# Moving the block sums and low parts of one stage to VectorE, and reordering loads at two stage borders, in a one-core mixer and feed-forward block

## The chip, the core and the metric

One core of a Trainium2 chip runs the whole program as one launch. The metric is device microseconds of one execution; the time before is the median of three runs, 1592.3 us (1587.58 to 1594.35). The instruction streams are TensorE (PE, with its weight loads as PEld), VectorE (DVE), ScalarE (ACT), GpSimd (POOL) and SyncE (SP). SP issues most loads and stores; POOL issues some as well. Each stream runs its own instructions strictly in the order in which they were written.

## What is computed

One layer over 1024 positions of width 1024. The reference, cut to what matters here:

```python
u = rms_norm(h, g_norm_mix)
proj = einsum('btd,de->bte', u, w_in) + b_in
mq, mk, mv, mo, mi, mf, nq, nkv, ngate, merge = split_columns(proj, IN_SIZES)
y_m = mlstm_mixer(mq, mk, mv, mo, mi, mf, ...)   # 4 heads of 128, conv of 4 taps, chunks of 128
y_n = nsa_mixer(nq, nkv, ngate, pe_cmp, ...)     # compressed, selected and window attention, 8 heads
branch = einsum('btnw,nwd->btnd', stack(y_m, y_n), w_branch)
h = h + sum_n(sigmoid(merge) * branch) @ w_out
f = rms_norm(h, g_norm_ffn)
h = h + (silu(f @ w_gate) * (f @ w_up)) @ w_down
return rms_norm(h, g_final)
```

Matrix products are done on pairs of float32r numbers, a high part (ACT copies the value in the shorter type) and a low part (value minus high part, one subtraction), as three products: high by high, high by low, low by high.

## The kernel before

The work has five stages; the times in brackets are those of the profiled execution.

**Stage A** (0 to 399 us) loads x, norms and transposes it, and computes all of the input projection but most of the merge columns, the four mLSTM heads, and the compressed keys and values. The projection goes pair by pair (`PAIRS`, twelve pairs of 256 output columns). Each pair takes seven block products instead of eight (a seven-product scheme): product 1, 2 and 4 take raw weight blocks, products 6, 7, 5 and 3 take sums and differences of blocks. `sums` (L741) forms these, `prep` (L767) makes the high part on ACT and the low part by `ew`, `product` runs 12 matmuls of 512 columns on PE, and `finish` (L797) adds the result into the output with the bias. For the query and key pairs `conv` (L838) adds the four taps: one ACT step and three DVE steps over 1024 columns. The activations' own block sums are made once by `forms` and `fsplit` (L599, L613), for j = 0 to 3.

Where `ew` is given `ANY` (L400), the step may go to DVE (one instruction, planned at 700 ns) or to POOL (two instructions of half the size, planned at 1800 ns); where it is given `V`, only to DVE.

`compress` (L1030) makes the compressed keys and values: for each of two inputs it loads four pieces of weights, adds the position rows to shifted windows (`windows`, L1047: four small additions for each piece, on DVE or POOL), and runs four small matmuls for each piece. `restore` (L1074) brings a part of the activations' parts back from memory by eight POOL loads, once product 4 of the last pair no longer needs their place. `head_load` (L1085), `values` (L1098), `mask`, `scale_q` and `core` (L1178) are the heads' recurrence. `merge_B` (L1270) fills PE beside them.

The order of stage A is worked out when the program is written: a planner (`Plan`, L64) keeps a clock for each engine, takes each step's cost and a delay for each DMA, and writes whichever step can start first; among steps that are ready it takes the lowest rank, which is the place in the program minus a boost. `load` (L406) holds the planner's picture of DMA: 1.5 us after the issue, big loads one after the other at 4 ns for each KB, POOL loads always 4.5 us.

**Stage C** (the attention from 413.7 to 736 us) goes with ten merge tiles of 48 matmuls as filler on PE, ordered by a second planner. Its keys, queries and bias rows are loaded by `load_pair` (L1354) from POOL: for the first pair of heads four loads of 256 KB for the queries (QA), eight of 256 KB for the keys (KH, KL), and four for bias rows (FB, FW). `behind(0)` (L1349) then copies the compressed keys behind them, also on POOL. The values (VHL, 2 MB, written out to memory in stage A) are loaded back by the step at L1299 to L1301, which the planner of stage A writes; so it stands in POOL's queue ahead of `load_pair(0)` (L1385). The pools of stage C reuse stage A's memory tile by tile.

**Stage D** (its branch products from 766.7 to about 860) multiplies both mixers' outputs by the branch weights and gates them. `load_y` (L1807) loads the twelve pieces of y (512 KB each) and makes their high parts on ACT and low parts on DVE; it runs step by step between the last two merge tiles, and what is left of it is run off before the first branch product. The first eight branch steps (`FIRST`, L1866) go over both halves and two column tiles for the first mixer, then the same for the second; `load_gates` (L1835) loads the merge gates, for the first four steps right before them.

**Stage E** (860 to the end) is the output projection and the feed-forward part, with the seven-product scheme again but a planner and an `ANY` of its own; the change does not touch it.

Of the kernel before, what the change touches and what calls it, by code (L numbers as in the profile page):

```python
# [14 lines left out]
P = 128  # L15
T = 1024
# [22 lines left out]
FB_ = 40  # L39
MA_ = (60, 60)  # L40
# [130 lines left out]
def body(ctx, tc, a, out, stop=None, dbg=None):  # L171
# [166 lines left out]
    with ExitStack() as sa:  # L338
# [67 lines left out]
        def load(eng, kb, parts, reads, writes, cost=450.0, after=0.0):  # L406

            q = {"SP": nc.sync, "ACT": nc.scalar, "Pool": nc.gpsimd}[eng]

            def go(e):  # L410
                for d_, s_ in parts:
                    q.dma_start(d_() if callable(d_) else d_, s_() if callable(s_) else s_)
                n = len(landed)
                if eng != "Pool":
                    if n >= 8:
                        st.end = max(st.end, landed[n - 8][0])
                    big = [x for x in landed if x[1]]
                    t = st.end + 1500.0
                    if kb > 100:
                        t = max([t] + [x[0] for x in big[-1:]]) + 4.0 * kb  # L420
                    landed.append((t, kb > 100))
                    st.lat = t - st.end
                else:
                    st.lat = 4500.0
            st = pA.step(((eng, cost),), go, reads, writes, after=after)
            return st
# [172 lines left out]
        def fsplit(q, j, src, reads):  # L599
            if q == 4:  # L600
                i = 2 * j + 1
                cs = slice(P * i, P * i + P)
                b = K(True, prior=[ub[i][0], ub[i][2]])
                hi, lo = UTH[:, 0:4, cs], UTL[:, 0:4, cs]
            else:
                b = K(True)
                hi, lo = (X[:, j, XI[q], z] for z in range(2))
                xform.append(b)
            fsb[q, j] = [b]
            act(630.0, lambda: hi, src, AF.Copy, reads, [b])  # L610
            ew(ANY, lambda: lo, src, lambda: cast32(hi), ALU.subtract, reads, [b])

        def forms(j):  # L613

            p12, p22 = ptb[2 * j + 1]
            fsb[3, j] = ub[2 * j + 1][1::2]
            ce, cs = (slice(P * n, P * n + P) for n in (2 * j, 2 * j + 1))
            us = ub[2 * j + 1][0::2]
            load("SP", 512, [(d_u[j][z], cast32((UTH, UTL)[z])[:, 0:4, cs]) for z in range(2)], us, [dub[j]])
            c, t1, t2, t4 = (piece(nm, z) for nm in ("g00", "g01") for z in range(2))  # L620
            at = lambda b: (lambda: four(b.ap))
            u_ = lambda t, kh: (lambda: cast32(t)[:, 4 * kh:4 * kh + 4, ce])
# [3 lines left out]
            ew(ANY, at(t1), at(t1), u_(UTL, 0), ALU.subtract, [l11], [t1])  # L626
            ew(V, at(t2), at(p22), at(t1), ALU.subtract, [p22, t1], [t2])
            ew(V, at(c), at(p22), at(c), ALU.subtract, [p22], [c])
            ew(ANY, at(t4), u_(UTH, 1), at(t2), ALU.subtract, [t2, h21], [t4])
            ew(ANY, at(t4), at(t4), u_(UTL, 1), ALU.add, [l21], [t4])  # L630
# [85 lines left out]

        PAIRS = [("n", 0), ("c", 0), ("q", 0), ("n", 1), ("k", 0), ("s", 0), ("q", 1), ("v", 0), ("k", 1), ("v", 1), ("o", 0), ("o", 1)]
# [23 lines left out]
        def sums(m, n):  # L741
# [5 lines left out]
            if n == 3:  # L747
                ew(ANY, h(r0, LO), h(r0, LO), h(r0, HI), ALU.subtract, (), [r0])
                o = (r0, h(r0, LO))
            elif n == 1:  # L750
                sums(m, 3)
                ew(ANY, h(r0, HI), h(r0, HI), h(r1, HI), ALU.add, [r1], [r0])
                o = (r0, h(r0, HI))
            elif n == 2:
                b = piece("x3", m % 2)
                ew(ANY, lambda: four(b.ap), h(r1, HI), sums(m, 3)[1], ALU.subtract, [r0, r1], [b])
                o = (b, lambda: four(b.ap))
            else:
                d, s2 = sums(m, 2)
                ew(ANY, h(r1, LO), h(r1, LO), s2, ALU.subtract, [d], [r1])  # L760
                o = (r1, h(r1, LO))
# [5 lines left out]
        def prep(m, q):  # L767
# [29 lines left out]
        def finish(m, blk, ps, other):  # L797
# [4 lines left out]
            pv, ov = (lambda: ps.ap), (lambda: other.ap)  # L802
            if kind in "qk":
# [4 lines left out]
                stt(800.0, lambda: par(flat(w.ap), r), lambda: four(ps.ap), bias, lambda: four(other.ap), ALU.add, ALU.add, [ps, other, b_c], [w])  # L808
# [6 lines left out]
            if kind == "o":  # L815
                ew(V, v, pv, ov, ALU.add, [ps, other], [x])
                stp("ACT", 630.0, lambda: nc.scalar.activation(x.ap, x.ap, AF.Sigmoid, bias=bias), [b_c, tabs[-1]], [x])
                store(256, [(par(d_mx["o"][j], r), lambda: four(x.ap))], x, dst["o", j])
            else:
                stt(760.0, v, pv, bias, ov, ALU.add, ALU.add, [ps, other, b_c], [x])  # L820
# [3 lines left out]
                else:  # L824
# [6 lines left out]
                    else:  # L831
                        ew(ANY, lambda: fr(x.ap), v, lambda: y.ap, ALU.subtract, [y], [x])
# [5 lines left out]
        def conv(m, col):  # L838
# [3 lines left out]
            pA.boost = -60  # L842
# [4 lines left out]
            for s in range(1, 4):  # L847
                stt(1700.0, lambda s=s: flat(c.ap)[:, s:T], lambda s=s: flat(w.ap)[:, 0:T - s], tap(3 - s), lambda s=s: flat(c.ap)[:, s:T], ALU.mult, ALU.add, [w], [c])
# [6 lines left out]
        def product(m, q, part=None):  # L855
# [28 lines left out]
            elif q == 5:  # L884
                finish(m, (1, 1), ps, v[3])
                add(v[2], v[2])
# [40 lines left out]
        seq += [(m, q) for m in range(2, NP - 1) for q in (1, 2, 6, 7, 5, 4, 3)]  # L927
        seq += [(NP - 1, q) for q in (1, 2, 4, 6, 7, 5, 3)]
# [101 lines left out]
        def compress(j):  # L1030
# [10 lines left out]
            for z in range(4):  # L1041
# [5 lines left out]
                def windows(e, z=z, fl=fl):  # L1047
                    for o in range(4 * z, 4 * z + 4):
                        ENG[e].tensor_scalar(fl()[:, o % 4], kx()[:, :, 2 * o:2 * o + 16 * 62 + 1:16], COLS[:, R_PE + 16 * j + o:R_PE + 16 * j + o + 1], None, ALU.add)
                pA.step((("DVE", 1700.0), ("Pool", 4000.0)), windows, [kb, b_c], [fb_])  # L1050
# [4 lines left out]
                stp("PE", 880.0, go, [fb_, wb], [ph])  # L1055
            stp("ACT", 330.0, lambda: nc.scalar.activation(hsv, ph.ap[:, 0:126], AF.Silu), [ph, tabs[-1]], [b_hs])
# [74 lines left out]
        for n, (m, q) in enumerate(seq):  # L1131
# [143 lines left out]
        head_load(0, "vo")  # L1275
# [22 lines left out]
        vh = {}  # L1298
        vb_ = K(None, keys=[(f"v{n}", z) for n in range(4) for z in range(2)], make=lambda: vh.setdefault("t", att.tile([P, NT, 4, P], F32R, name="VHL", tag="VHL")))  # L1299
        load("Pool", 2048, [(lambda: vb_.ap.rearrange("p i n c -> p (i n c)"), d_vh)], [b_dvh], [vb_], cost=700.0)  # L1300
# [9 lines left out]
        VHL = vh["t"]  # L1310
# [75 lines left out]
    behind(0)  # L1386

# [414 lines left out]
    with ExitStack() as se:  # L1802
# [4 lines left out]
        def load_y():  # L1807

            ring = [q1_tile(n, F32)[:, 2 * z:2 * z + 2, :].rearrange("p a c -> p (a c)") for n in (4, 0, 1) for z in range(2)]
            ys, loads = {}, 0  # L1810
            for k in range(10):
                ys[k] = []
                for src in ([d_ym[k]] if k < 4 else [d_yn[0][k - 4], d_yn[1][k - 4]]) if k < 8 else []:
                    ys[k].append(ring[loads % 6])
                    loads += 1
                    nc.sync.dma_start(ys[k][-1], src[:, :])
                if k > 1:
                    y, *more = ys.pop(k - 2)
                    for y2 in more:
                        nc.vector.tensor_tensor(y, y, y2, ALU.add)  # L1820
                    for half in range(2):
                        hs = slice(512 * half, 512 * half + 512)
                        split_evict(YH[:, k - 2, hs], YL[:, k - 2, hs], y[:, hs])
                yield

        ly = load_y()
        for j in range(NMB + NMX + NMC, 16):
            for z, _ in enumerate(merge_tile(j, gring, psD, 8)):
                if z % 2 == 1:
                    next(ly, None)  # L1830
        for _ in ly:
            pass
        sgs = {}
# [7 lines left out]
        wide = Pieces([q1_tile(n, F32)[:, z, :] for n in (5, 3) for z in range(4)])  # L1841
        gring, narrow = wide, gring
# [24 lines left out]
        for d, half, b in FIRST[:4]:  # L1867
            load_gates(d, half)
        for n, (d, half, b) in enumerate(FIRST):
# [10 lines left out]
            if n == 5:  # L1880
                gring = narrow
                gring.n = 0
                load_gates(2, 0)
        for d in range(2, 8):
# [625 lines left out]
```

## Time and profile before

| | before |
|---|---|
| median of 3 runs | 1592.3 us (1587.58 to 1594.35) |
| the profiled execution | 1597.51 us, its span 1595.7 us |
| busy in the span | PE 97%, DVE 72%, ACT 49%, POOL 19% |
| mean granted TensorE clock | 0.985 |

A page of the profile gives busy time by engine, the span in 40 slices, the chain that ended last, and the costliest groups. Other views used here: the waits (who waited for whom, summed), a table of stretches (busy time of each engine between two moments, with the granted clock), the timeline of one engine, groups by line, and the DMA issues with their time to landing. L with a number is a line of the kernel; `wOwhi<-rA,wOwhi` reads "writes wOwhi from rA and wOwhi", where whi and wlo name buffers of a ring that holds high and low parts, rA, Rg, RG and XR are buffers of stage A, X the activations' sums, and PSA its PSUM banks. XB is the memory of X in its second use. A busy PE is not PE at its peak.

### The profile page before, as it was taken

What the parts mean: (1) busy time and instruction counts of PE and PEld (TensorE: products, weight loads), DVE (VectorE), ACT (ScalarE), POOL (GpSimd) and SP (SyncE); (2) the same over time, 40 slices, a digit from 0 to 9 for tenths busy, and PEclk for the clock granted to TensorE, in tenths of its full rate; (3) what the DMA queues carried; (4) which work ended last, traced back from release to release, by engine and by line L of the source; (5) the groups of instructions that cost most, each with busy time, mean ns of one, the idle gap of its engine ahead of it and who ended that gap; (6) DMA issues with size and microseconds to landing.
All of it is one profiled execution on the core that took longest, in us unless ns stands there. A gap on an engine that the chain in (4) does not pass through costs nothing.

```text
span 1595.7 us, 22548 instructions
## 1 busy us (share of the span) xinstructions
PE 1545.5 (97%) x7810; PEld 1304.5 (82%) x7810; DVE 1149.9 (72%) x2334; ACT 779.6 (49%) x1677; POOL 304.9 (19%) x435
## 2 busy tenths in 40 slices
PE   9899999999699999999799999999999999999997
PEld 7777878888599989898688888888888888888886
DVE  6987777546498968884565678666666666988996
ACT  6533333366488868884444454333333333454443
POOL 4767665422211221101002000000000000000130
PEclk9999999999799999999899999999999999999999
DMA  7446774694722452216546423322222223741302
GB/s 205 162 128 206 214 240 130 165 267 156 158 67 90 87 136 67 83 41 204 169 143 209 137 89 123 102 83 79 80 79 79 81 91 100 283 167 45 106 1 106
DMA packets 169980, 205.86 MB, mean 129 GB/s; under 512 B 10345, under 2 KB 128391, under 8 KB 169610
## 3 DMA queue, kind: packets, MB, share of 16 engines
q1 hardware_dynamic: 156584, 179.43, 36.2%
q0 software_dynamic: 12992, 24.67, 6.6%
q8 instruction: 61, 1.00, 0.3%
q14 instruction: 53, 0.43, 0.1%
q10 hardware_dynamic: 290, 0.33, 0.1%
HBM read 149.77 MB, written 62.48 MB: 133 GB/s over the span
## 4 chain that ended last, share of the span: by engine, by line
PE 83%; DMA 7%; DVE 4%; ACT 2%; issue 2%; POOL 1%; SPq 1%; DVEq 0%; POOLq 0%; ACTq 0%
PE PS L287 14%; PE PS L288 14%; PE PS L286 14%; PE T L1504 4%; PE PSA L286 4%; PE PSA L288 4%; PE PSA L287 4%; PE d L286 2%; PE d L288 2%; PE d L287 2%; PE obank L1524 2%; PE obank L1526 2%; PE br L286 2%; PE br L287 2%; PE br L288 2%
## 5 line engine op out<-in xcount | busy, mean ns | idle before, releaser
L1942 DVE TENSOR_TENSOR sl<-PS,sl 128x512 f32<-128x512 f32 x182 | 123.6, 689 | 100.9 <-PE PS L288 100.5
L1942 POOL TENSOR_TENSOR acc<-acc 128x512 f32<-128x512 f32 x6 | 9.2, 1549 | 617.6 <-DVE acc L1942 617.6
L1513 DVE TENSOR_TENSOR TL<-T,TH 128x512 fp32r<-128x512 f32 (+1 forms) x184 | 103.1, 582 | 33.3 <-ACT TH L1509 32.1
L1942 DVE TENSOR_TENSOR sl<-sl,sl 128x512 f32<-128x512 f32 (+1 forms) x130 | 88.6, 688 | 22.9 <-DMA d_h<-sl 7.2
L1509 ACT ACTIVATE TH<-T 128x512 fp32r<-128x512 f32 (+1 forms) x184 | 90.1, 510 | 29.9 <-PE T L1504 27.3
L1945 ACT ACTIVATE sl<-sl 128x512 f32<-128x512 f32 (+1 forms) x77 | 48.5, 632 | 58.0 <-PE PS L287 34.4
L1524 PE MATMUL obank<-TH,VHL 128*128 128x256 f32 x264 | 75.4, 309 | 0.0
L286 PE MATMUL d<-UTH,whi 128*128 128x512 f32 x176 | 71.9, 409 | 1.0 <-ACT mg L1341 0.7
L288 PE MATMUL d<-UTH,wlo 128*128 128x512 f32 x176 | 69.1, 393 | 0.0
L287 PE MATMUL d<-UTL,whi 128*128 128x512 f32 x176 | 69.0, 392 | 0.0
L1526 PE MATMUL obank<-TL,VHL 128*128 128x256 f32 x264 | 68.0, 281 | 0.0
L286 PE MATMUL PS<-q 128*128 128x512 f32 x172 | 66.9, 389 | 0.0
L287 PE MATMUL PS<-q 128*128 128x512 f32 x172 | 66.9, 389 | 0.0
L288 PE MATMUL PS<-q 128*128 128x512 f32 x172 | 66.9, 389 | 0.0
L263 POOL TENSOR_TENSOR wlo<-raw,whi 128x256 fp32r<-128x256 f32 x44 | 31.1, 737 | 184.8 <-ACT whi L257 154.4
L288 PE MATMUL PSA<-UTH,wOwlo 128*128 128x512 f32 x164 | 64.8, 395 | 1.3 <-POOL wOwlo L441 1.3
L286 PE MATMUL PSA<-UTH,wOwhi 128*128 128x512 f32 x156 | 63.8, 409 | 0.0
L1945 ACT ACTIVATE q<-sl 128x512 fp32r<-128x512 f32 x74 | 43.1, 623 | 42.3 <-PE PS L287 32.2
L287 PE MATMUL PSA<-UTL,wOwhi 128*128 128x512 f32 x156 | 60.9, 390 | 0.0
L286 PE MATMUL br<-YH,whi 128*128 128x512 f32 x128 | 50.9, 398 | 8.2 <-ACT whi L257 8.2
L1945 ACT ACTIVATE wh<-sl 128x512 fp32r<-128x512 f32 x39 | 24.6, 631 | 58.2 <-PE PS L287 40.8
L1526 PEld LDWEIGHTS obank<-TL,VHL 128*128 128x128 f32 x264 | 50.0, 189 | 1.1 <-DVE TL L1513 0.3
(1396 smaller groups left out, 5088.8 us busy)
## 6 DMA issues: line engine op xcount, KB each, us to landing
d_gu<-sl SPq DMA_DIRECT2D x44, 256.0 KB, 2.2
rA<-in_w_in SPq DMA_DIRECT2D x18, 512.0 KB, 5.7
q<-d_mg SPq DMA_DIRECT2D x32, 256.0 KB, 3.5
d_rep<-d_row POOLq DMA_DIRECT2D x8, 960.0 KB, 7.2
sl<-in_w_down SPq DMA_DIRECT2D x15, 512.0 KB, 3.5
sl<-d_gu SPq DMA_DIRECT2D x15, 512.0 KB, 4.8
ra<-in_w_gate SPq DMA_DIRECT2D x14, 512.0 KB, 3.9
ra<-in_w_up SPq DMA_DIRECT2D x13, 512.0 KB, 4.8
```

What stands on the lines that cost most here:

```text
L263: nc.gpsimd.tensor_tensor(lo[:, zs], v[:, zs], cast32(hi)[:, zs], ALU.subtract)
L286: nc.tensor.matmul(ps, ah, bh, start=first, stop=False)
L287: nc.tensor.matmul(ps, ah, bl, start=False, stop=False)
L288: nc.tensor.matmul(ps, al, bh, start=False, stop=last)
L1504: nc.tensor.transpose(pt[:, z, P * r:P * r + P], e, ident)
L1509: nc.scalar.activation(hl[0][:, 0:m], pt[:, 0:m], AF.Copy)
L1513: nc.vector.tensor_tensor(hl[1][:, 0:m], pt[:, 0:m], cast32(hl[0])[:, 0:m], ALU.subtract)
L1524: nc.tensor.matmul(po, vv, th[:, z, :], start=(st[1] == 0), stop=False)
L1526: nc.tensor.matmul(po, vv, tl[:, z, :], start=False, stop=(st[1] == st[2]))
L1942: return pl.step(alts, lambda e: ENG[e].tensor_tensor(out_(), x(), y(), alu), reads, writes, **kw)
L1945: return pl.step((("ACT", cost),), lambda e: nc.scalar.activation(out_(), x(), fn), reads, writes, **kw)
```

## The change

Five things are edited.

1. In stage A the block sums of the weights, the low parts of all products and of one output, and the activations' sums for j = 2 and 3 go to DVE alone (`V` in place of `ANY`). The low parts of merge weights and of the first value tiles keep their choice.
2. The additions of `windows` go to ACT, two instructions a step, and the compress steps get a lower rank (boost -120). The first five `prep` calls get a boost of 100, product 5's last sum one of 100, and `conv` -120 in place of -60.
3. The planner's picture of DMA changes: 2.2 us after 30 us for SP, 4.5 for POOL, big loads at 3 ns for each KB, and POOL's big loads share the line with SP's.
4. Product 4 of the last two pairs is taken together, earlier, so `restore` can start earlier. The first head's v is loaded earlier. At the border to stage C the attention's loads go first and the values' reload last.
5. At the border to stage D the loads and the splitting of y are put at written places among the last two merge tiles (`plan_y`), with two of the eight left until after the first two branch steps; the gates of the first column tile are loaded during the last merge tile, into a ring of their own.

```diff
@@ load (stage A's planner)
-                if eng != "Pool":
-                    if n >= 8:
-                        st.end = max(st.end, landed[n - 8][0])
...
+                t = st.end + (1500.0 if st.end < 30000.0 else 2200.0 if eng != "Pool" else 4500.0)
...
+                    t = max([t] + [x[0] for x in big[-1:]]) + (4.0 if st.end < 30000.0 else 3.0) * kb
@@ fsplit, forms
-            ew(ANY, lambda: lo, src, lambda: cast32(hi), ALU.subtract, reads, [b])
+            ew(ANY if j < 2 else V, lambda: lo, src, lambda: cast32(hi), ALU.subtract, reads, [b])
@@ sums (four such lines)
-                ew(ANY, h(r0, LO), h(r0, LO), h(r0, HI), ALU.subtract, (), [r0])
+                ew(V, h(r0, LO), h(r0, LO), h(r0, HI), ALU.subtract, (), [r0])
@@ prep
+            pA.boost = PB_ if nop[0] <= 4 else 0
             act(630.0, lambda: four(b.ap[:, 0, :]), src, AF.Copy, [r], [b])
-            ew(ANY, lambda: four(b.ap[:, 1, :]), src, lambda: cast32(four(b.ap[:, 0, :])), ALU.subtract, [r], [b])
+            ew(V, lambda: four(b.ap[:, 1, :]), src, lambda: cast32(four(b.ap[:, 0, :])), ALU.subtract, [r], [b])
+            pA.boost = 0
@@ order of the products
-        seq += [(m, q) for m in range(2, NP - 1) for q in (1, 2, 6, 7, 5, 4, 3)]
-        seq += [(NP - 1, q) for q in (1, 2, 4, 6, 7, 5, 3)]
+        seq += [(m, q) for m in range(2, NP - 2) for q in QO]
+        seq += [(NP - 2, q) for q in QO if q not in (3, 4)]
+        seq[-1:] = [(NP - 2, 4), (NP - 1, 4), seq[-1], (NP - 2, 3)] + [(NP - 1, q) for q in QO if q != 4]
@@ compress
-                        ENG[e].tensor_scalar(fl()[:, o % 4], kx()[:, :, 2 * o:2 * o + 16 * 62 + 1:16], COLS[...], None, ALU.add)
-                pA.step((("DVE", 1700.0), ("Pool", 4000.0)), windows, [kb, b_c], [fb_])
+                        nc.scalar.activation(fl()[:, o % 4], kx()[:, :, 2 * o:2 * o + 16 * 62 + 1:16], AF.Identity, bias=COLS[...])
+                pA.boost = -WB_
+                for o0 in (4 * z, 4 * z + 2):
+                    stp("ACT", 720.0, lambda o0=o0, windows=windows: windows(o0), [kb, b_c], [fb_])
@@ heads
+            if (m, q) == (NP - 2, 7):
+                head_load(0, "v")
...
-        head_load(0, "vo")
+        head_load(0, "o")
@@ the values' reload
-        load("Pool", 2048, [(lambda: vb_.ap.rearrange("p i n c -> p (i n c)"), d_vh)], [b_dvh], [vb_], cost=700.0)
         core(3)
...
     load_pair(0)
     behind(0)
+    nc.gpsimd.dma_start(VHL.rearrange("p i n c -> p (i n c)"), d_vh[:, :])
@@ stage D
+        plan_y = {(0, 0): [lambda: load_y(0, 1, 2, 3)], (0, 2): [lambda: load_y(4)], (0, 8): [lambda: split_y(0)],
+                  (0, 10): [lambda: split_y(1), lambda: load_y(5)], (0, 13): [lambda: split_y(2)], (1, 1): [lambda: split_y(3), lambda: load_y(6)],
+                  (1, 7): [lambda: split_y(4), lambda: load_y(7)], (1, 12): [lambda: split_y(5)]}
...
+                if (n, z) == (1, 9):
+                    gring, late = early, gring
+                    for half in range(2):
+                        load_gates(0, half)
+                    gring = late
...
-        for d, half, b in FIRST[:4]:
-            load_gates(d, half)
+        for half in range(2):
+            load_gates(1, half)
...
+                gate(d, half, b, *x)
+                split_y(6)
+                continue
+            if n == 1:
+                gate(d, half, b, *x)
+                split_y(7)
+                continue
```

In `plan_y` the key (1, 7) stands for the second of the two tiles, after its eighth group of three matmuls.

More of the change, by code (lines that the diff above doesn't have):

```diff
@@ L39 @@
 FB_ = 40
+PB_ = 100
+UB_ = 100
+CB_ = 120
+WB_ = 120
 MA_ = (60, 60)
@@ L413, in go @@
                 n = len(landed)
-                if eng != "Pool":
-                    if n >= 8:
-                        st.end = max(st.end, landed[n - 8][0])
[L417 to L420, printed above, removed]
+                t = st.end + (1500.0 if st.end < 30000.0 else 2200.0 if eng != "Pool" else 4500.0)
+                if eng != "Pool" and n >= 8:
+                    t = max(t, landed[n - 8][0])
+                big = [x for x in landed if x[1]]
+                if kb > 100:
+                    t = max([t] + [x[0] for x in big[-1:]]) + (4.0 if st.end < 30000.0 else 3.0) * kb
+                if eng != "Pool" or kb > 100:
                     landed.append((t, kb > 100))
-                    st.lat = t - st.end
-                else:
-                    st.lat = 4500.0
+                st.lat = t - st.end
             st = pA.step(((eng, cost),), go, reads, writes, after=after)
@@ L802, in finish, with total @@
             pv, ov = (lambda: ps.ap), (lambda: other.ap)
+            def total(cost, view, x):
+                o = (lambda: four(other.ap)) if kind in "qk" else ov
+                stt(cost, view, (lambda: four(ps.ap)) if kind in "qk" else pv, bias, o, ALU.add, ALU.add, [ps, other, b_c], [x])
             if kind in "qk":
@@ L807, in finish @@
                 w = wt[m, col]
-                stt(800.0, lambda: par(flat(w.ap), r), lambda: four(ps.ap), bias, lambda: four(other.ap), ALU.add, ALU.add, [ps, other, b_c], [w])
+                total(800.0, lambda: par(flat(w.ap), r), w)
                 if (m, col, 1 - r) in wt:
@@ L816, in finish @@
                 ew(V, v, pv, ov, ALU.add, [ps, other], [x])
-                stp("ACT", 630.0, lambda: nc.scalar.activation(x.ap, x.ap, AF.Sigmoid, bias=bias), [b_c, tabs[-1]], [x])
+                stp("ACT", 630.0, lambda: nc.scalar.activation(x.ap, x.ap, AF.Sigmoid, bias=bias), [ps, b_c, tabs[-1]], [x])
                 store(256, [(par(d_mx["o"][j], r), lambda: four(x.ap))], x, dst["o", j])
             else:
-                stt(760.0, v, pv, bias, ov, ALU.add, ALU.add, [ps, other, b_c], [x])
+                total(760.0, v, x)
                 if kind in "cv":
@@ L1309, in body @@
         ws.nd, ws.ns = NMB + 2, NMB + 1
-        VHL = vh["t"]
+        VHL = att.tile([P, NT, 4, P], F32R, name="VHL", tag="VHL")
         VHC, KHC, KLC = (cmp_view(x) for x in ("v", "kh", "kl"))
@@ L1806, in body, with load_y, split_y @@
         YL = dp.tile([P, 8, T], F32R, name="YL")
[L1807 to L1811, printed above, removed]
+        ring = [q1_tile(n, F32)[:, 2 * z:2 * z + 2, :].rearrange("p a c -> p (a c)") for n in (4, 0, 1) for z in range(2)]
+        ys, sgs = {}, {}
+        def load_y(*kk):
+            for k in kk:
                 ys[k] = []
-                for src in ([d_ym[k]] if k < 4 else [d_yn[0][k - 4], d_yn[1][k - 4]]) if k < 8 else []:
-                    ys[k].append(ring[loads % 6])
-                    loads += 1
+                for src in [d_ym[k]] if k < 4 else [d_yn[0][k - 4], d_yn[1][k - 4]]:
+                    ys[k].append(ring.pop(0))
+                    ring.append(ys[k][-1])
                     nc.sync.dma_start(ys[k][-1], src[:, :])
[L1817 to L1833, printed above, removed]
+        def split_y(k):
+            y, *more = ys.pop(k)
+            for y2 in more:
+                nc.vector.tensor_tensor(y, y, y2, ALU.add)
+            for half in range(2):
+                hs = slice(512 * half, 512 * half + 512)
+                split_evict(YH[:, k, hs], YL[:, k, hs], y[:, hs])
         def load_gates(d, half):
@@ L1866, in body @@
         FIRST = [(d, half, b) for b in range(2) for d in range(2) for half in range(2)]
-        for d, half, b in FIRST[:4]:
-            load_gates(d, half)
+        for half in range(2):
+            load_gates(1, half)
         for n, (d, half, b) in enumerate(FIRST):
@@ L1880, in body @@
             if n == 5:
-                gring = narrow
                 gring.n = 0
+                gring, late = early, gring
                 load_gates(2, 0)
+                gring = late
         for d in range(2, 8):
```

37 lines of the change are left out of this document (21 added, 16 removed).

## The prediction

> **What bounds the kernel now.** I read the page first, then a table of stretches, PE's waits, and then the places that these name.
>
> ```profile
> span 1595.7 us, 22548 instructions
> PE 1545.5 (97%) x7810; PEld 1304.5 (82%) x7810; DVE 1149.9 (72%) x2334; ACT 779.6 (49%) x1677; POOL 304.9 (19%) x435
> ```
>
> PE is the bound as a whole, and the change adds and removes no matmul. So it can win only time in which PE stands still or runs slowly. The table of stretches (stretch, length, busy time and instructions of PE, PEld, DVE, ACT and POOL, granted clock, DMA share, GB/s) shows where that is:
>
> ```profile
> 40.00:100.00 60.00, 53.48 (x268) 44.23 (x267) 56.26 (x94) 28.22 (x54) 46.17 (x59) 0.97 0.44 138
> 100.00:340.00 240.00, 231.11 (x1067) 190.83 (x1066) 158.71 (x211) 93.66 (x158) 134.42 (x156) 0.98 0.70 199
> 340.00:401.80 61.80, 61.18 (x394) 53.81 (x393) 38.08 (x114) 40.00 (x149) 15.62 (x24) 1.00 0.57 184
> 401.80:423.70 21.90, 8.60 (x25) 6.27 (x25) 3.85 (x25) 2.62 (x13) 8.38 (x19) 0.61 1.08 231
> 736.00:758.50 22.50, 22.50 (x100) 18.30 (x98) 9.28 (x13) 9.48 (x16) 2.83 (x4) 1.00 0.86 306
> 758.50:771.90 13.40, 5.16 (x13) 3.98 (x13) 5.70 (x8) 6.31 (x10) 2.80 (x4) 0.62 0.58 194
> ```
>
> PE is idle for 15.4 us between 40 and 340, and hardly at all in the 62 us behind that; then come two borders at which it is mostly idle and at a low clock. PE's waits name the causes (us in total, times, longest):
>
> ```profile
> PE S0w L1422 <- POOL KH L1352: 11.9, 1, 11.9
> PE br L286 <- ACT whi L257: 8.2, 1, 8.2
> PE PSA L1107 <- DMA XB<-d_mv: 3.3, 1, 3.3
> PE PSA L288 <- DVE wOwhi L438: 2.8, 1, 2.8
> ...
> PE PSA L1054 <- DMA VW<-in_w_cmp: 2.2, 2, 1.8
> ...
> PE PSA L288 <- POOL wOwlo L441: 1.3, 1, 1.3
> ```
>
> A wait costs more than itself, since the clock falls behind it (stretches right behind three waits):
>
> ```profile
> 159.74:164.30 4.56, 4.56 (x17) 3.83 (x18) 1.45 (x2) 1.15 (x2) 3.04 (x5) 0.63 1.10 279
> 332.75:338.40 5.65, 5.65 (x27) 5.65 (x28) 0.96 (x3) 2.47 (x8) 0.00 (x0) 0.50 0.82 254
> 413.70:423.70 10.00, 8.58 (x24) 6.27 (x25) 3.85 (x25) 2.62 (x13) 4.00 (x11) 0.50 0.53 173
> ```
>
> So the 1.8 us wait for compress weights costs 4.56 x 0.37 = 1.7 more, and the 3.3 us wait at 332.75 costs 5.65 x 0.5 = 2.8 more: 6.1 in all. I use 6.1 below as the price of one such wait.
>
> **The border to the attention.** POOL's timeline (start, length, what; in brackets the idle time before it and its releaser), and one DMA issue:
>
> ```profile
> 389.81 0.58 POOL L412 DMA_DIRECT2D VHL<-d_vh  x1 [22.04 <-ACT XR L1219]
> 390.39 2.10 POOL L1360 DMA_DIRECT2D QA<-d_q  x4
> ...
> 412.53 0.54 POOL L1381 DMA_DIRECT2D FW<-d_rep  x1 [2.55 <-DMA KL<-d_kl]
> 413.07 0.62 POOL L1352 CAST KH<-CMP 128x512 fp32r<-128x512 f32 x1
> VHL<-d_vh POOLq DMA_DIRECT2D x1, 2048.0 KB, 9.4
> ```
>
> POOL stands idle for 22 us before the values' load, with all the attention's loads queued behind it; then these travel behind its 2 MB; POOL waits for landings between its later issues (the FW row shows one); and the copy behind the keys, which releases PE, is last (413.07 + 0.62 = 413.7, and PE had waited 11.9, so since 401.8). In 21.9 us PE does 8.60 us at half clock, that is 4.3 us of full-speed work: 21.9 - 4.3 = 17.6 us are lost.
>
> With the values last, the loads start when their memory is free. The code puts it where XB (head 1) was; when that is free the trace does not show. It is between POOL's last work of the stage (389.81 - 22.04 = 367.8) and 389.81. Sixteen loads took 413.07 - 390.39 = 22.7 us to be issued with the values in front, so about 22.7 - 9.4 = 13.3 without. From 367.8 they end at 381, from 389.81 at 403.1 against PE's arrival at 401.8. What is late next is VHL, issued after the copies and landing 9.4 later:
>
> ```profile
> 426.28 0.36 PE L1524 MATMUL obank<-TH,VHL 128*128 128x256 f32 x1
> ```
>
> This first use came 12.6 us after the copy (426.28 - 413.7); 8.6 of those us were PE work at half clock, so at full clock I estimate 12.6 - 4.3, about 8. If VHL is issued by 400 it lands by 409.4, when PE wants it at 401.8 + 8 = 410: nothing is lost. If the copies end at 403.1 + 1.2 = 404.3, PE starts 2.5 late and finds VHL, landing at 413.7, 1.4 after it wants it; with half the clock lost for 5 to 6 us behind that, as in the row of 332.75, 7 are lost. POOL's small memsets and the next merge tile's low part queue behind its issue. Gain 10 to 17.6; I take **15**, nearer to the early start, since POOL is idle through all of the 22.04 us.
>
> **The border to stage D.** ACT's timeline and the loads' row:
>
> ```profile
> 743.71 1.16 ACT L282 ACTIVATE YH<-q 128x512 fp32r<-128x512 f32 x2 [5.24 <-DMA q<-d_ym]
> ...
> 765.65 1.04 ACT L257 ACTIVATE whi<-raw 128x1024 fp32r<-128x1024 f32 x1
> q<-d_yn SPq DMA_DIRECT2D x8, 512.0 KB, 6.7
> ```
>
> ACT waits for one y after the other (the first wait begins at 743.71 - 5.24 = 738.5), and the branch weights' high part (765.65) stands behind the last y, which the first products don't even read. Loss: 13.4 - 5.16 x 0.5 = 10.8 us. In the new order that high part is written after the fourth y, and the first four branch steps need only y 0 to 3. They are 48 matmuls, 10.8 us at the merge tiles' 22.5/100. Twelve y loads are 6 MB; at the 306 GB/s of the tiles' stretch they take 20 us from 738.5, and even a whole landing time of 6.7 later is 765, before 758.5 + 10.8 = 769.3, when the second mixer's y is first read. The later y loads wait in SP's queue for their slots, with the next branch weights behind them, which are split only after the second branch step. What is late next is ACT at the second column tile: its weights' high part waits behind a sigmoid of gates that are loaded behind y: 0 to 3 us. Gain 7.5 to 10.8; I take **9**.
>
> **Stage A.** First, `restore` and the first head's v start earlier. Landing times of the transfers beside the 332.75 wait:
>
> ```profile
> UTH<-d_u POOLq DMA_DIRECT2D x4, 256.0 KB, 9.0
> XB<-d_mk SPq DMA_DIRECT2D x1, 512.0 KB, 10.0
> ```
>
> 2 MB of `restore` shared the DMA engines with head 1's loads. With product 4 of the last pair eight products from the end rather than four, it starts four products earlier, 48 matmuls, about 11 us, longer than its landing time; and on POOL it now holds up only head 0's mask, since the low parts have left that queue. The head's v, moved up in SP's queue, can hold the raw weights behind it only until its slot is free, which the trace doesn't show: nothing to one wait of 6.1, taken as nothing, since the transfer takes the place of one that stood in the crowd. So the wait for head 1 should go: 6.1, or nothing if the planner, told shorter delays, only asks sooner. Second, the compress windows leave DVE and POOL, and their matmuls give way to products: the waits of 2.2 and their 1.7 of clock go or stay. Third, POOL's low parts that PE waited for (1.3) go.
>
> Against this stands DVE's load. POOL's part in `ew` and in the windows, and rows that price it:
>
> ```profile
> 40.00:100.00 60.00, 44.97 (x54) 0.97 0.44 138
> 100.00:340.00 240.00, 80.02 (x91) 0.98 0.70 199
> L1049 POOL TENSOR_SCALAR VW<-VW,COLS 128x126 f32<-128x126 f32 x20 | 20.5, 1038 | 10.1 <-DMA VW<-d_kc 10.1
> L1056 ACT ACTIVATE MSC<-PSA 128x126 f32<-128x126 f32 x2 | 0.5, 267 | 0.5 <-PE PSA L1054 0.5
> 74.27 2.30 POOL L441 TENSOR_TENSOR RG<-RG,UTL 128x256 f32<-128x256 f32 x2
> 74.78 1.21 DVE L438 TENSOR_TENSOR rA<-rA,rA 128x512 f32<-128x512 f32 x1
> 76.51 0.68 DVE L438 TENSOR_TENSOR wOwhi<-rA,wOwhi 128x512 fp32r<-128x512 f32 x1
> ```
>
> The first two rows are L441 alone: POOL busy and count. Two such instructions become one DVE instruction of 0.68. After 100 that is 91/2 x 0.68 = 31 us more on DVE, 158.7 + 31 = 190 of 240: it fits. Between 40 and 100 about 40 of the 54 move (the others are for j below 2 and the first values): 20 x 0.68 = 13.6, so 56.3 + 13.6 = 69.9 of 60 us, if nothing gets cheaper. But beside POOL a DVE subtraction takes 1.21 instead of 0.68. If each POOL instruction lengthened one DVE instruction by 0.53, taking away 40 saves 21; if half of them, 10.6, and DVE comes to 59.3 of 60. So DVE is full there, between 49 and 70. ACT takes 32 windows of 0.27, 8.6 us beside 94 busy of 240: free. Gain of stage A: 6.1 + 2 + 1.3 of the waits, less 1.4 for a DVE that is full in places, **8**, between -6 (10 us too many on DVE, 4 gained) and 14 (all of these waits, the 2.8 for wOwhi too: 6.1 + 2.2 + 1.7 + 1.3 + 2.8).
>
> **The sum.** 15 + 9 + 8 = 32 us. Against the profiled execution's 1597.5 (span 1595.7) this gives 1565.5; that execution lies 5.2 above the median of the runs, so against 1592.3 the forecast is **1560.3 us**. With all lower bounds the gain is 11.5 (1581), with all upper ones 42.4 (1550).
>
> **The rivals.**
>
> *VHL takes the wait's place.* PE writes its order ahead, so it stops at the first VHL product. With the latest issue this border gains its lower bound, 10, and the sum is 27: 1565.3. For it: 9.4 us of landing against 8 of work. Chance 0.13.
>
> *The loads collide.* 4.7 MB of attention's loads (12 of 256 KB, bias rows of 2 x 512 and 2 x 320 KB by their shapes) move into the end of stage A, where merge weights and the last head are still loaded; as at 332.75, one such wait costs 6.1: 1566.4. The rows of 9.0 and 10.0 speak for it; against it, the DMA engines are busy for a share of 0.57 between 340 and 401.8, so there is room.
> The Trainium skill's page "DMA: Bandwidth & Descriptors", section "Issuing engines are not separate DMA queues", says that transfers started by any engine run on the same 16 DMA engines and interleave; this speaks against the early loads, and the rows of 9.0 and 10.0 agree. Chance 0.10.
>
> *DVE is full from 40 to 100.* 70 us of work for 60, PE late by 10: stage A loses 6, the sum is 15 + 9 - 6 = 18: 1574.3. Chance 0.14.
>
> *Given back, no change.* Deferred compress weights stand in SP's queue waiting for their slot, with the next pair's raw weights behind them; four such waits at 6.1 are 24.4, all that the borders give, and stage A gains nothing else: about 1592. Chance 0.08.
>
> *Slower: low parts behind the convolution.*
>
> ```profile
> L448 DVE SCALAR_TENSOR_TENSOR RG<-Rg,COLS,RG 128x1023 f32<-128x1023 f32 (+2 forms) x24 | 34.4, 1433 | 5.1 <-ACT RG L846 4.9
> ```
>
> Eight convolutions put three steps of 1.43 on DVE, 4.3 us. Now POOL can make low parts meanwhile; then all must queue. If the parts are ready less than 4.3 us ahead, PE (2.7 us a product) stops each time for up to 4.3 and loses 1.7 of clock: 8 x 6 = 48. Then 1592.3 - 24 + 48 = 1616. Against it: the planner ranks the convolution 120 steps back, and the ring holds four products' parts. Chance 0.10.
>
> **How the numbers follow.** Forecast 0.45, rivals 0.13, 0.10, 0.14, 0.08, 0.10. Half a per cent (8 us) is about what a measurement of this kernel can tell from no change. The forecast and the first three rivals are faster by more than that: 0.82; no change with 0.08; slower 0.10. The range, 1549 to 1582, takes in both sets of bounds and holds those first four cases.
>
> **What would show it.** Right: no wait at S0w, QA issued before 389, VHL last; br starts within 2 us of the last merge tile; clock 1.00 at both borders; no wait at values of head 1; DVE subtractions at 0.68 and POOL nearly silent from 60 to 300. Wrong: PE waits for wOwhi or wOwlo from DVE, above all beside L448 on 1021 to 1023 columns; a PE wait on VHL; raw weights landing late.

## The result, and the profile after

The changed kernel takes 1580.19 us (median of 5 runs, 1575.32 to 1580.72) beside 1592.66 for the kernel before (5 runs, 1587.58 to 1594.35): a ratio of 0.9919, with a 95% interval of 0.9897 to 0.9941. It is faster by 12.5 us, where 32 were forecast. The profiled execution took 1580.19 us.

The page of the changed kernel:

```profile
span 1578.4 us, 22429 instructions
PE 1536.5 (97%) x7810; PEld 1300.7 (82%) x7810; DVE 1153.7 (73%) x2380; ACT 793.3 (50%) x1713; POOL 174.4 (11%) x291
```

PE runs the same 7810 matmuls and POOL has lost 131 us of work. The table of stretches has the same columns as before (stretch, length, busy time and instructions of PE, PEld, DVE, ACT and POOL, granted clock, DMA share, GB/s); the third row lies within the second, and the last two are the borders:

```profile
40.00:100.00 60.00, 54.49 (x274) 45.99 (x273) 54.05 (x110) 31.09 (x58) 21.08 (x33) 0.94 0.43 137
100.00:136.00 36.00, 21.02 (x81) 16.85 (x80) 12.91 (x21) 6.42 (x12) 2.27 (x5) 0.76 1.00 304
130.40:136.00 5.60, 5.60 (x13) 4.42 (x14) 4.74 (x8) 3.33 (x6) 0.00 (x0) 0.50 1.03 323
136.00:340.00 204.00, 201.08 (x946) 167.92 (x945) 153.09 (x217) 93.68 (x161) 26.74 (x34) 1.00 0.62 175
340.00:399.00 59.00, 58.74 (x397) 52.61 (x396) 35.95 (x116) 43.74 (x168) 18.16 (x29) 1.00 0.94 229
399.00:416.40 17.40, 14.97 (x80) 12.34 (x79) 9.05 (x37) 7.85 (x27) 5.98 (x16) 1.00 0.71 254
747.90:760.60 12.70, 10.01 (x36) 7.46 (x35) 4.69 (x7) 5.22 (x7) 0.00 (x0) 0.87 0.85 298
```

Both borders are much fuller than before: PE works for 15.0 of 17.4 us at full clock at the first, and for 10.0 of 12.7 at 0.87 at the second. The row to look at is the second: in 36 us of stage A, PE works for 21, at a clock of 0.76, with the DMA engines full (share 1.00). Nothing like it stood in the kernel before. PE's waits say the same (us in total, times, longest):

```profile
PE PSA L292 <- DVE wOwlo L440: 15.8, 2, 15.0
PE PSA L541 <- DVE XR L450: 4.7, 1, 4.7
PE PSA L1122 <- DMA XB<-d_mv: 2.9, 1, 2.9
PE br L290 <- ACT whi L261: 2.2, 1, 2.2
PE obank L1539 <- DMA VHL<-d_vh: 1.4, 1, 1.4
```

A single wait of 15.0 us for a low part on VectorE is new. (The 4.7 us for XR stand at 45 us; the kernel before waits 2.7 there. No run here asks why.) Since both kernels issue 7810 matmuls, progress can be compared by counting them: the time at which the n-th matmul starts in the changed kernel, minus that in the kernel before (start in the kernel before in brackets).

| matmul | difference, us |
|---|---|
| 550 (114.9) | -0.6 |
| 600 (126.2) | +17.3 |
| 1200 (264.3) | +7.6 |
| 1900 (393.0, end of stage A) | +4.5 |
| 1950 (418.1, attention) | -10.8 |
| 4000 (731.5) | -10.6 |
| 4200 (786.9, stage D) | -16.7 |
| last | -17.3 |

The borders gave 15.3 and 6.1 us. Stage A lost 17.9 at one place, which is the wait of 15.0 and the half clock of 5.6 us behind it (5.6 x 0.5 = 2.8), and won about 13 elsewhere. (The two profiled executions lie 17.3 apart, the medians 12.5: the prediction noted that the first is 5.2 above its median.)

What happened at that place shows in four views of the changed kernel. First POOL's timeline:

```profile
96.44 1.73 POOL L416 DMA_DIRECT2D MSC<-d_S  x1 [1.73 <-DMA d_S<-RG]
98.16 3.59 POOL L416 DMA_DIRECT2D d_rep<-d_row  x7
103.95 0.52 POOL L416 DMA_DIRECT2D d_rep<-d_row  x1 [2.20 <-DMA MSC<-d_S]
```

`d_rep` are the attention's bias rows: for each of the eight heads one row is copied to 128 rows in memory, 960 KB in one DMA (L1130 before, L1145 after; the change doesn't touch the line). The planner gives each a starting time 14 us after the last, but that is only the place in POOL's order: on the chip POOL goes on as soon as its instruction before is done. Now nothing but one wait of 2.20 us stands between them, and eight times 960 KB leave within 6.3 us. In the kernel before, POOL's low parts stood between, and the issues went from 118.1 to 229.4. The DMA issues between 85 and 135 (KB each, median us to landing), with the row of POOL's queue (packets, MB, share of the 16 engines):

```profile
q0 software_dynamic: 1296, 7.91, 51.2%
...
d_rep<-d_row POOLq DMA_DIRECT2D x8, 960.0 KB, 19.1
rA<-in_w_in SPq DMA_DIRECT2D x3, 512.0 KB, 25.8
...
d_q<-Rg SPq DMA_DIRECT2D x2, 256.0 KB, 17.5
Rg<-in_w_in SPq DMA_DIRECT2D x1, 512.0 KB, 26.5
```

The same in the kernel before, between 80 and 150:

```profile
d_rep<-d_row POOLq DMA_DIRECT2D x2, 960.0 KB, 7.8
...
d_q<-Rg SPq DMA_DIRECT2D x5, 256.0 KB, 2.6
Rg<-in_w_in SPq DMA_DIRECT2D x2, 512.0 KB, 6.2
```

SP's stores and raw weights take four to seven times as long. The Trainium skill's page "DMA: Bandwidth & Descriptors", section "Issuing engines are not separate DMA queues", says that transfers of all issuing engines share the same 16 DMA engines and interleave; these rows agree, the burst being POOL's and the delay SP's. Last, SP's and VectorE's timelines:

```profile
106.54 18.98 SPq L416 DMA_DIRECT2D d_q<-RG  x1
```

```profile
128.96 0.75 DVE L450 SCALAR_TENSOR_TENSOR Rg<-PSA,COLS,XR 128x512 f32<-128x512 f32 x1 [21.71 <-DMA d_q<-Rg]
129.63 0.68 DVE L440 TENSOR_TENSOR wOwlo<-rA,wOwlo 128x512 fp32r<-128x512 f32 x1
```

VectorE is not overloaded: it stands idle for 21.71 us, until the store of the buffer that it is to write next has landed. The low part for PE is queued behind that instruction. So PE's row "waits for DVE wOwlo" names the last link; the first is a queue on an engine with no work.

### The profile page after: what moved, and what is told of

Its sections match the earlier page's. It is cut to its first block, busy times and chain, and to the rows that moved or that the text cites. A ratio compares the mean times of both kernels' runs of the same rounds, so it can differ in the third digit from the quotient of the medians.

```text
span 1578.4 us, 22429 instructions
## 1 busy us (share of the span) xinstructions
PE 1536.5 (97%) x7810; PEld 1300.7 (82%) x7810; DVE 1153.7 (73%) x2380; ACT 793.3 (50%) x1713; POOL 174.4 (11%) x291
## 4 chain that ended last, share of the span: by engine, by line
PE 89%; DMA 5%; DVE 3%; ACT 1%; issue 1%; SPq 0%; POOL 0%; DVEq 0%; ACTq 0%; POOLq 0%
PE PS L291 14%; PE PS L290 14%; PE PS L292 14%; PE PSA L292 6%; PE PSA L290 6%; PE PSA L291 6%; PE T L1519 4%; PE d L290 3%; PE d L292 3%; PE d L291 3%; PE obank L1539 2%; PE obank L1541 2%; DMA d_q<-Rg 2%; PE br L292 2%; PE br L291 2%; PE br L290 2%
## 5 line engine op out<-in xcount | busy, mean ns | idle before, releaser
L1539 PEld LDWEIGHTS obank<-TH,VHL 128*128 128x128 f32 x264 | 49.8, 189 | 2.6 <-ACT TH L1524 1.6
L292 PE MATMUL br<-YH,wlo 128*128 128x512 f32 x128 | 50.5, 395 | 0.5 <-DVE wlo L269 0.5
```

Source lines behind the costliest of these rows:

```text
L292: nc.tensor.matmul(ps, al, bh, start=False, stop=last)
L1539: nc.tensor.matmul(po, vv, th[:, z, :], start=(st[1] == 0), stop=False)
```

## The experiments

Each time is the median of four to twelve runs, and each ratio is to the kernel before, run beside it: 1591.14 us for the first four experiments, 1590.99 for the next four, 1590.93 for the last. The changed kernel had 1592.66 beside it. Differences between two versions are of their medians as they stand; where the two were not run beside each other, 1 to 2 us of such a difference can be that drift.

**late6**: the changed kernel; six broadcasts leave in attention, behind VHL, and every other instruction keeps its place.

```diff
-            load("Pool", 983, [(d_rep[h], d_row[h, :].partition_broadcast(P))], (), [K(True)], cost=700.0, after=...)
+            load("Pool", 983, [(d_rep[h], d_row[h, :].partition_broadcast(P))] if h < 2 else [], (), [K(True)], cost=700.0, after=...)
...
     nc.gpsimd.dma_start(VHL.rearrange("p i n c -> p (i n c)"), d_vh[:, :])
+    for h in range(2, NH): nc.gpsimd.dma_start(d_rep[h], d_row[h, :].partition_broadcast(P))
```

> The changed kernel with six of the eight bias broadcasts (d_rep of heads 2 to 7, 960 KB each) issued behind the values' reload in attention; every other instruction keeps its order. Theory (burst): in the changed kernel POOL has nothing left to do between the eight broadcasts, issues them back to back at 98 to 104, and they hold the DMA engines to 129.5; stores and raw weights behind them land 17 to 26 us after issue, and PE's 14.98 us wait for wOwlo plus the half clock behind it is that. Then the wait goes to under 1 us, stores at 100 land within 6 us again, and the time falls by 15 to 18 us, to 1562 to 1565. Rival (VectorE alone is too much): the low parts of stage A queue up on VectorE, the broadcasts only lie beside; then the wait at 130 stays over 10 us and the time is 1578 to 1582. Second rival (the new order of branch loads puts the raw weights late): the stores get quick again but raw weights still come late; 1570 to 1578.

1562.06 us, ratio 0.9821 (0.9804 to 0.9837): 18.1 us below the changed kernel, or 16.6 with each taken against the kernel before beside it; the profiled executions lie 18.8 apart. PE's longest wait for a low part in this kernel, and the stretch of the burst:

```profile
PE PSA L292 <- DVE wOwlo L440: 0.8, 1, 0.8
```

```profile
98.00:130.00 32.00, 32.00 (x143) 26.51 (x142) 25.10 (x39) 11.19 (x18) 0.00 (x0) 1.00 0.78 228
```

PE works through all 32 us, with VectorE busier (25.1 us against 9.12 in the changed kernel). This decides for the burst and against VectorE as the bound. (The first store of 256 KB behind the two broadcasts that are left lands after 9.9 us, not within the 6 that were expected, and PE does not wait for it.) The six broadcasts now lie together at 385.6 to 388.2, as a burst again, and cost nothing there: the difference to the kernel before stays at -30.5 from matmul 2000 to 4000. What a burst costs depends on what waits behind it.

**late4**: the same with `h < 4`, so that four stay in the burst.

> As the run with six late broadcasts, but only four (heads 4 to 7) are issued in attention, so four remain in the burst. Burst theory: one takes 3.35 us of the DMA engines, so four hold them to about 115 instead of 129.5; PE had work until 115.4, so a wait of 0 to 4 us is left and the time is 1562 to 1569, most of the gain with half of the traffic moved, since the burst costs only what outlasts the products in stock. If the cost went with the number of broadcasts, half of the gain: 1571 to 1573. VectorE rival: 1578 to 1582.

1567.21 us, ratio 0.9853 (0.9832 to 0.9873): 13.0 of 18.1 us won, where late6 moved six broadcasts and this moves four. Its four runs lie in two pairs, at 1564 to 1565 and at 1569 to 1570. The time alone does not tell how the cost grows: in proportion to the broadcasts moved it would be 18.1 x 4/6 = 12.1, as near to 13.0 as the theory. (The expectation set half of the gain against the theory, as if late6 had moved all eight.) The waits tell the two apart: at the place of the burst PE waits 15.0 us with eight broadcasts in it, 3.4 with four (at 116.4, with half clock behind it) and not at all with two; in proportion it would be 7.5 and 3.8. So the cost is what outlasts PE's stock of products.

**burst_before**: the kernel before; the first broadcast's step issues all eight.

```diff
-  [(d_rep[h], d_row[h, :].partition_broadcast(P))]
+  [(d_rep[x], d_row[x, :].partition_broadcast(P)) for x in range(NH) if h == 0]
```

> The kernel before, with all eight broadcasts issued back to back on POOL where the first stood (at 118); PE, VectorE, ScalarE and SP keep every instruction in order. Burst theory: the DMA engines are held for 27 us (8 times 3.35), loads and stores of 118 to 145 land 15 to 25 us after issue instead of 3 to 8, and PE waits 8 to 18 us between 135 and 165; the time rises to 1600 to 1611. VectorE rival: with the low parts still on POOL the burst costs at most its 3.6 us of issue time on POOL, 1592 to 1597.

1597.06 us, ratio 1.0041 (1.0025 to 1.0057): slower by 6 us. That misses the theory's 1600 to 1611 and lies at the upper end of the rival's 1592 to 1597. The trace decides: the wait is there, behind the broadcasts and as long as the theory had it:

```profile
PE PSA L288 <- POOL wOwhi L441: 11.1, 1, 11.1
```

Against the kernel before it is 13.0 us late at matmul 700, 7.3 at 800 and 3.75 at 1200: PE meets everything later, and the waits that the kernel before has at 149.7 to 160 and at 231 to 237, with the half clock at 161, are not there any more. A new wait ahead of old ones is paid partly by them. (At the last matmul this profiled execution is 1.1 us ahead of that of the kernel before, which was 5 us slower than its median, so the 6 us rest on the medians.) In the changed kernel nothing was paid back: against late6 it is 19.5 us late at matmul 600 and 18.8 at the last.

**any_after**: the changed kernel with `ANY` again for the sums and low parts (`V` back to `ANY` in `fsplit`, `forms`, `sums`, `prep` and the one output).

> The changed kernel with the low parts, block sums and form sums of the pairs allowed on POOL again (as before), everything else changed. POOL's own work then stands between the broadcasts again. Burst theory: the broadcasts go out one at a time over about 100 us, the wait at 130 goes, and the time is 1562 to 1570: what is left against the run with six late broadcasts (1 to 5 us) is what VectorE alone is worth by itself. VectorE rival: 1562 to 1570 too, but with no change in the landing of stores if the broadcasts were not the cause. If the burst comes from the new model of loads alone, the broadcasts stay together and the time stays at 1578 to 1582.

1565.33 us, ratio 0.9852 (0.9831 to 0.9874). The broadcasts leave one at a time again:

```profile
L416 POOL DMA_DIRECT2D d_rep<-d_row x8: 521/533/540, 112.3 to 207.5; - x8
```

The stores of d_q from Rg land after 3.5 us, against 17.5 in the changed kernel. So the step that the change is named for made it 15 us slower (13 with each taken against the kernel before beside it), by emptying POOL.

**any_late6**: any_after and late6 together.

> The changed kernel with low parts and sums allowed on POOL again AND six broadcasts issued in attention: against the run with six late broadcasts it differs only in the engine of the low parts and sums (and the order that the plan makes of it), and so measures VectorE alone with the broadcasts out of the way. If VectorE alone is worth something by itself: 1564 to 1567, as with the broadcasts between POOL's steps. If the 3 us by which that run was slower came from the broadcasts in stage A: 1561 to 1563. If VectorE alone is a loss by itself: under 1560.

1566.77 us, ratio 0.9846 (0.9827 to 0.9866). Against late6 it is 4.7 us slower: with the broadcasts out of the way VectorE alone is the better choice, by 3 to 5 us. Spread out in stage A the broadcasts cost nothing (any_after took 1565.33).

**values_last**: the kernel before, with the values' reload moved behind `load_pair(0)` and `behind(0)` and nothing else.

```diff
-        load("Pool", 2048, [(lambda: vb_.ap..., d_vh)], [b_dvh], [vb_], cost=700.0)
+        load("Pool", 2048, [], [b_dvh], [vb_], cost=700.0)
...
     behind(0)
+    nc.gpsimd.dma_start(VHL.rearrange("p i n c -> p (i n c)"), d_vh[:, :])
```

> The kernel before, with one part of the change alone: the values' reload (2 MB) is issued behind all loads of the first pair of heads; nothing else moves. Theory: the 11.92 us wait for the first keys at 413.7 and the half clock behind it were the reload standing ahead on POOL's queue and in the DMA engines; the trace of the changed kernel gained 15.3 us between the end of stage A and the first scores, so this alone gives 13 to 17 us, 1574 to 1578. Rival (the gain at that border needs the other parts too, since the loads go only as early as stage A's buffers come free): the values then arrive late in turn, PE waits for them 5 to 9 us, and the time is 1582 to 1588.

1577.86 us, ratio 0.9919 (0.9903 to 0.9935): 13.1 us faster alone, as much as the whole change brings. The stretch in which the kernel before did 8.60 us of work at 0.61:

```profile
401.80:423.70 21.90, 20.54 (x126) 17.67 (x125) 17.80 (x71) 15.56 (x51) 2.29 (x10) 1.00 0.42 144
```

**branch_order**: the kernel before with stage D's part of the diff alone (part 5).

> The kernel before, with the other order of the branch loads and splits (stage D) alone. The forecast put 9 us on this part; the trace of the changed kernel shows 6.0 us at this border, because 2.2 and 0.5 us of waits for the second column tile and a half clock behind them are left. Theory (the forecast's term is too large by what is left): 5 to 7 us faster, 1584 to 1587. Rival (the term is worth 9 in full where stage A is undisturbed): 1581 to 1583. Rival (it only shifts): 1590 to 1592.

1586.22 us (twelve runs, 1582.11 to 1590.66), ratio 0.9972 (0.9958 to 0.9987): 4.8 us faster (2 to 7 by the interval). The wait for whi shrinks from 8.2 to 2.5 us and doesn't go.

**late6_split**: late6, and the second column tile's weights are split ahead of the first gates' sigmoid.

```diff
                 W[d] = ws.get(j_br[d])
+                ws.split(j_br[1])
             x = branch(d, half, b)
             if n == 0:
-                ws.split(j_br[1])
                 ws.dma(j_br[2])
```

> The run with six late broadcasts, and in stage D the second column tile's weights are split on ScalarE ahead of the first gates' sigmoid instead of behind it. Theory: at the start of stage D PE waits 3.85 us for whi, since ScalarE stands at a sigmoid whose gates are still on their way and the split is queued behind it; then the wait and the half clock behind it (1.7 us) go, 4 to 6 us, 1556 to 1558. Rival (the raw weights themselves come late): no change, 1561 to 1563. Rival (the sigmoid becomes late instead and products wait for their buffers): 1560 to 1563.

1558.34 us, ratio 0.9798 (0.9780 to 0.9816): 3.7 us below late6, a little less than the 4 to 6 expected. In late6 PE's wait for this whi is 3.9 us. ACT's timeline in the changed kernel shows why:

```profile
752.55 1.28 ACT L1866 ACT_TABLE_LOAD   x1 [3.95 <-DMA q<-d_mg]
753.84 0.63 ACT L1866 ACTIVATE q<-q 128x512 f32<-128x512 f32 x1
754.38 1.04 ACT L261 ACTIVATE whi<-raw 128x1024 fp32r<-128x1024 f32 x1
```

ScalarE stood idle for 3.95 us at a sigmoid whose gates were on their way, with the split that PE needed queued behind. A wait of 1.2 us for the last y is left.

**late6_split_v**: late6_split, and head 1's four loads leave SP with the values first (SP's order is shown; nothing else moves).

```diff
-  XB<-d_M, XB<-d_mq, XB<-d_mk, XB<-d_mv
+  XB<-d_mv, XB<-d_M, XB<-d_mq, XB<-d_mk
```

> The run with six late broadcasts and the earlier split, and in stage A the four loads of head 1 (gate sums, queries, keys, values) leave SP in the order values first instead of values last; every other instruction keeps its order. The forecast said that the wait for the values at 332.75 of the kernel before goes since the loads behind the last products start earlier; it is still 2.5 to 3.2 us long in all kernels. Theory: it is the place in SP's queue and in the DMA engines, four loads of 512 KB issued within 4 us of which the one that PE needs first lands last, 10 us after its issue; then the values land 3 to 5 us earlier, the wait of 2.71 us falls below 1 us with the half clock behind it, and the time falls by 2 to 5 us, to 1553 to 1556. Rival (the next thing that PE needs is one of the other three loads): the wait moves to the gate sums' mask and the time stays at 1557 to 1560.

1556.43 us (1555.25 to 1557.88), ratio 0.9783 (0.9770 to 0.9796): 1.9 us below late6_split, just short of the 2 to 5 that were expected, and the runs of the two overlap (late6_split: 1557.02 to 1560.38), so that the time alone does not show the gain. In the profile the wait for the values is gone, and two of 0.7 and 0.5 us for recurrence steps came in its place:

```profile
XB<-d_mv SPq DMA_DIRECT2D x1, 512.0 KB, 4.1
```

```profile
PE PSA L1231 <- ACT Rg L1219: 0.7, 1, 0.7
...
PE PSA L1122 <- ACT Rg L1219: 0.5, 1, 0.5
```

With this it is the fastest version of the study, 34.5 us below the kernel before and 23.8 below the changed one; PE is busy for 99% of its span.

## Why the forecast gain was too large

The direction was right. The sum, 32 us, was not, mainly for one step. That 1580.19 still lies in the range of 1549 to 1582 is luck: stage A came out near its lower bound of -6, for a reason that was not in that bound, and the border to stage D below its own of 7.5.

**What failed: stage A, forecast at 8 us of gain.** Its text counted the low parts that leave POOL as busy time of VectorE, and listed "POOL nearly silent from 60 to 300" among the signs that it is right. It did not ask what else stood in POOL's order between those low parts, and so put the cost of POOL's other issues at nothing. Eight broadcasts stood there, and the low parts had kept them apart. Sent together they cost 18.1 us (late6). The sign "raw weights landing late" and "PE waits for wOwlo from DVE" did show, but for a reason that none of the rivals named: *The loads collide* had the mechanism, at another place and with other transfers.

Apart from that the stage did better than forecast. Of late6's 29.1 us (1591.14 - 1562.06), 13.1 and 4.8 are the two borders by their own runs, so that stage A without the burst is worth some 11, if the parts add up; by the counted matmuls it is 15.6 at the end of the stage, against a profiled execution of before that is long by 5.2. With the burst, 11 - 18.1 = -7 where +8 stood; the counted matmuls give -4.5 for the two profiled executions. (This is a division of the measured total, since the 11 is what the other runs leave, and no check of it.)

**DVE full from 40 to 100** (rival at 0.14) did not happen. VectorE was put between 49 and 70 us of 60, and it came to 54.05. L438 before and L440 after, alone, in that stretch (length, busy time and count):

```profile
40.00:100.00 60.00, 37.74 (x46) 0.97 0.44 138
```

```profile
40.00:100.00 60.00, 37.39 (x59) 0.94 0.43 137
```

Thirteen more instructions take no more time: 0.63 us on average instead of 0.82, with most of POOL's work out of the way. It is not the mix of shapes: the five instructions `RG<-RG,UTL` on 128x512 take 1025 ns on average before and 692 after, while the seven `RG<-PSA,RG`, which read one operand from PSUM, take 683 in both. The forecast's two cases of this relief gave 49 and 59 of 60 us, and 54 lies between them. The convolutions (slower rival) held nothing up either: the changed kernel has no wait of PE behind one.

**The wait for head 1's values** (6.1 of the 8) did not go. `restore` did start earlier, POOL's first issue of it at 307.27 (310.51 before) in spite of 7.6 us of delay, but it was not the cause: the wait is 2.5 to 3.3 us in every kernel up to late6_split. The four loads stood in SP's queue behind a store that waits for ScalarE, and the one that PE needs first landed last. With the order turned round the wait is gone. In the changed kernel the wait is 2.9 us but no half clock follows, so that some 3 of the 6.1 came all the same: its matmul 1400 is 7.6 us late against the kernel before, its matmul 1600 only 4.3. When the half clock follows such a wait is taken up in the last section.

**The border to attention**, forecast at 15: 15.3 by the counted matmuls, 13.1 alone. The loads started when the forecast's middle had it, and the first scores do not wait. POOL's timeline:

```profile
377.28 2.15 POOL L1374 DMA_DIRECT2D QA<-d_q  x4 [5.87 <-ACT Rg L1219]
...
403.54 0.54 POOL L1395 DMA_DIRECT2D FW<-d_rep  x1 [14.95 <-PE PSA L1282]
...
405.19 0.53 POOL L1401 DMA_DIRECT2D VHL<-d_vh  x1
```

The rival *VHL takes the wait's place* had its condition in full: POOL stood for 14.95 us in front of one bias row whose memory was not free, and VHL left only at 405.19. It cost 1.4 us and no clock, not 5, since PE had products to do until then.

**The border to stage D**, forecast at 9: 6.1 by the counted matmuls, 4.8 alone. The residue that the forecast named (the second column tile's weights behind a sigmoid, 0 to 3 us) was real, 2.2 + 0.5 us, and half clock for 3.4 us behind it makes 1.7 more: 4.4. The sum allowed 1.8 for it (10.8 less 9), though the text said which instruction would be late. Moving that instruction gave 3.7, in late6, where it was later still.

## What to carry to other kernels

When work leaves an engine that also issues transfers, list what that engine issues between the removed instructions: they had been the pacing, and a planned start time holds nothing apart unless an instruction waits. Read a long wait for one engine back to the first idle link; here "PE waits for VectorE" was VectorE waiting for a store, and that for a burst of another queue. And a transfer's price is set by its place: the same six broadcasts cost 17 to 18 us among stores that buffers wait for, and nothing in attention.

## What the runs showed of the hardware

The price of a wait in clock is not fixed, as the prediction's 6.1 had it. Right behind a wait of 2.47 us in late6 and one of 2.71 in late6_split, at the same place:

```profile
318.49:322.49 4.00, 4.00 (x33) 3.88 (x34) 1.25 (x4) 2.70 (x10) 0.00 (x0) 1.00 1.02 327
```

```profile
318.93:322.40 3.47, 3.47 (x17) 3.47 (x18) 0.54 (x2) 2.02 (x7) 0.00 (x0) 0.51 0.95 301
```

The one costs nothing more, the other 1.7 us (3.47 x 0.49). In burst_before a wait of 3.20 us at this place is followed by full clock too (336.43 to 341.00: 1.00), so the length of the wait alone does not decide.

The Trainium skill's page "TensorE: Matmul & The Clock Gate", section "Part 1: The HAM clock gate (the "warmup" mystery)", says that the clock is judged over a window of about 3.4 us that runs freely, and that it falls after one idle window or more. The traces agree with the window: within the program the clock changes only on a grid of 3.41 us (in late6_split it is halved from 318.98 to 322.39, in the kernel before from 160.90 to 164.31 and from 331.56 to 338.39). They do not agree that the whole window has to be idle. Laid along that grid, the 2.71 us of late6_split fall into one step (315.56 to 318.98), and the half clock starts with the next; in the kernel before 1.84 us of idle time within one step (157.48 to 160.90) were enough. The 3.20 us of burst_before are split into 1.56 and 1.64 over two steps, the 2.47 of late6 into 1.89 and 0.59, and no half clock follows. So it matters how a wait falls on the grid. Over the eleven traces, from 13 us on, each of the 30 steps at full clock in which PE stood idle for 1.95 us or more is followed by half clock, and none with less than 1.5 us is (the program's end left aside); in between both occur. That is a count over traces; no run moved a wait along the grid to test it.

In the burst one issue instruction of SP took 18.98 us (the row at 106.54), where the two before it took 0.38 and 0.37. The same store takes 6.17 us in late4, with four broadcasts ahead of it, and 1.88 in late6, with two. So a burst on one queue can hold the engine that issues on another; how it does so, the traces do not show.
